# Seven half-size products in place of eight in the first feed-forward matmul of a transformer block

## The chip, the cores and the metric

The kernel runs on one core of a Trainium2 chip. Its time is the device time of one execution in microseconds (us). Five engines of the core work side by side, each with an instruction queue of its own: TensorE (PE: matrix products; PEld: the loads of its stationary operand), VectorE (DVE), ScalarE (ACT), GpSimd (POOL), and SyncE (SP), which here issues the transfers between DRAM and the on-chip memory SBUF. Products are summed in PSUM, eight banks of 128 partitions by 512 numbers of four bytes.

## The reference, cut to what matters

The program is two transformer blocks on 512 tokens of width 1024. The part that changes is at the end of the second block:

```python
D_MODEL = 1024; SEQ = 512; D_FF = 4 * D_MODEL

def second_block(x, c, ..., w1, w2, w_ada, b_ada):
    ...
    x = x + gt1 * (mixed @ w_o[l])
    h = rmsnorm_2(x, g_norm2[l]) * (1.0 + sc2) + sh2
    x = x + gt2 * (jnp.square(jax.nn.relu(h @ w1[l])) @ w2[l])
    return x
```

So `h` is 512 x 1024, `w1` is 1024 x 4096 and `w2` is 4096 x 1024. The product `h @ w1` is the first feed-forward product.

## The kernel before, in words

All dense products are made to float32 accuracy from operands split in two: `split` (L130) copies a raw tile into a type with fewer bits (`act.copy`, ScalarE, L131), the high part, and subtracts it from the raw one (L128), the low part; the subtraction is on GpSimd by default, or on VectorE. `mm3` (L149) then issues three matmuls per 128 rows of the contraction: high by high, high by low, low by high (L150 to L152).

The second block keeps the tokens in columns: the normed input `h` lies as `hh`/`hl`, eight slices of 128 channels by 512 tokens, in tiles of the tags `QK` (high) and `PT` (low). The stage around the change runs so:

- `rows_second` (L694) ends the attention's output product for the second half of the tokens. Its last weight tiles use the buffers `wh`/`wl`, of which there are three each; raw weights land in `wr`, four buffers. In its middle, `col_norm` (L657) transposes the normed first half of the tokens on TensorE (L664), scales and shifts it (L668 on ScalarE, L670 on VectorE), and splits it (L672, L673).
- `norm2` (L1095) adds the residual to the second half (L1104, L1105), sums squares (L1106), forms the root (L157 to L161) and scales the rows (L1110) into four tiles of the tag `T`, which has five buffers.
- Meanwhile TensorE multiplies the first half of the tokens, 256 columns, with four of the first `EARLY` = 5 weight tiles (`first_half`). A weight tile is 1024 rows by 128 columns of `w1`: 8 x 3 = 24 matmuls. Then it transposes the second half, multiplies the fifth tile with the first half, and all five with the second half.
- The other 27 weight tiles are run whole, 512 columns, by `mtile` (L389); after each, `hid_out` (L1132) applies Relu and Square on ScalarE and writes the result to `hid`, 32 slices of 128 by 512, which are kept for the second product. Every second tile, `ada_step` (L257) does one step of the modulation vector on VectorE (L217, two operations on 512 KB of `w_ada`).

```python
    def hid_out(ft, srcs):
        t1 = tmp([128, 512])
        n = 512 // len(srcs)
        for i, ps in enumerate(srcs):
            s = slice(n * i, n * i + n)
            act.activation(t1[:, s], ps[:, :n], AF.Relu)
        act.activation(hid[ft], t1, AF.Square)
```

The order on TensorE is that of the program's text. The other engines' queues are ordered by a planner when the program is built: it takes the operation that is ready first by its own costs, and among ready ones the one that stands first in the text. All queues are worked off in order. Tiles of one tag share that tag's buffers; a tile waits until an earlier one's last reader is done. A bank of PSUM (`bank()`, eight) is treated as one thing: a write waits for reads of the same bank that stand before it.

Of the kernel before, what the change touches and what calls it, by code (L numbers as in the profile page):

```python
# [16 lines left out]
D = 1024  # L17
# [34 lines left out]
def hybrid_then_adaln_block(ctx, tc, a, out, tap=None):  # L52
# [1038 lines left out]
    h3h = [wt([128, 4, 512], "QK", F32R) for _ in range(2)]  # L1091
    h3l = [wt([128, 4, 512], "PT", F32R) for _ in range(2)]
# [22 lines left out]
    for t in range(4):  # L1115
        x = resid.tile([128, D], F32, name="xr", tag="xr", bufs=4)
        sp.dma_start(x, y1_d[128 * t:128 * t + 128, :])
        xr.append(x)
    us = norm2(hts[0], pss_o)
    pss = rows_second(hts[1], a["w_o_2"], x_of, kept2,  # L1120
                      lambda: col_norm(hts[0], us, h3h, h3l, scl[:, 2, :], mod[:, 24:32]))
    us = norm2(hts[1], pss)
    if tap: tap("x2", xr[2]); tap("h3", f(h3h[1][:, 1, :]))
    hh, hl = h3h, h3l

    hid = []
    for tag, n in [("PT", 1), ("V", 1), ("Y", 4), ("h", 2)]:
        for _ in range(n):
            t = wt([128, 4, 512], tag) if tag != "h" else hpool.tile([128, 4, 512], F32, name="hid", tag="h", bufs=4)
            hid += [t[:, q, :] for q in range(4)]  # L1130

    def hid_out(ft, srcs):  # L1132
        t1 = tmp([128, 512])
        n = 512 // len(srcs)
        for i, ps in enumerate(srcs):
            s = slice(n * i, n * i + n)
            act.activation(t1[:, s], ps[:, :n], AF.Relu)
        act.activation(hid[ft], t1, AF.Square)
# [3 lines left out]
    EARLY = 5  # L1142
    w1y = [wt([128, 2, KT, 128], "Y", F32R) for _ in range(2)]
    first = [weights([wcols(w1x, FF, 128 * ft, 128)], [KT, 128],
                     *((w1y[0][:, ft], w1y[1][:, ft]) if ft < 2 else (None, None))) for ft in range(EARLY)]
    halves = [bank() for _ in range(EARLY)]

    def first_half(ft, q):
        for k in range(KT):
            h, l = h_of(k, 256 * q, 256)  # L1150
            mm3(halves[ft][:, 256 * q:256 * q + 256], first[ft][0][:, k, :], first[ft][1][:, k, :], h, l, k == 0, k == KT - 1)
# [79 lines left out]
```

## Time and profile before

| | |
|---|---|
| three runs | 1066.61, 1068.08, 1071.96 us; median 1068.08 us |
| the profiled execution | 1064.9 us |
| its span, from the first to the last instruction | 1063.1 us |
| TensorE, its weight loads | busy 1027.0 us (97%), 845.1 us (79%) |
| VectorE, ScalarE, GpSimd | busy 527.6, 527.2, 309.2 us |
| mean granted clock of TensorE | 0.997 |

"Busy" is the time in which an engine has an instruction under way. Matmuls overlap: a row of 256 columns lasts 0.28 us, but the next one starts earlier, so the cost of one is read from the starts. Times within the trace count from the start of the span. "Granted clock" is the share of TensorE's full clock, 2.4 GHz, that it was given: 1.00 or 0.50.

### The profile page before, as it was taken

Reading aid. Unit: us, or ns where it says so; the run is one execution under the profiler, and the core shown is the slowest. Engines: PE = TensorE matmul, PEld = TensorE weight load, DVE = VectorE, ACT = ScalarE, POOL = GpSimd, SP = SyncE. Lnnn points to the kernel's source line nnn. Section 1 sums busy time; section 2 is a strip of 40 time slices with the busy share of each in tenths; the row PEclk is TensorE's granted clock in tenths of the full one; section 3 lists DMA queues with packets and bytes.
Section 4 is the critical chain, followed back from the end, with each engine's and each line's share of the span. In section 5 each row is a group of like instructions: output and inputs, shape, how many; then the busy total and the mean of one; then the engine's idle time right before and its main releaser. Section 6 shows DMA issues by size and latency. Waiting matters only on the chain.

```text
span 1063.1 us, 14244 instructions
## 1 busy us (share of the span) xinstructions
PE 1027.0 (97%) x5431; PEld 845.1 (79%) x5431; DVE 527.6 (50%) x1017; ACT 527.2 (50%) x990; POOL 309.2 (29%) x163
## 2 busy tenths in 40 slices
PE   7999999999999998999899988999999999999998
PEld 6987987778888887987678766798888888888886
DVE  5375866873534478368777587471131003121115
ACT  6365654554544554566687686354433433222221
POOL 4221123423332552112212115113322333323330
PEclk9999999999999999999999999999999999999999
DMA  8342532454633656236412235434445233233312
GB/s 239 84 119 64 151 114 80 139 141 121 175 98 95 237 160 210 71 99 165 134 50 61 70 107 151 156 100 119 119 122 153 82 100 113 87 99 97 100 60 80
DMA packets 133976, 125.48 MB, mean 118 GB/s; under 512 B 6054, under 2 KB 110338, under 8 KB 133907
## 3 DMA queue, kind: packets, MB, share of 16 engines
q1 hardware_dynamic: 133906, 124.56, 39.8%
q8 instruction: 43, 0.70, 0.3%
q14 instruction: 27, 0.21, 0.1%
HBM read 119.82 MB, written 4.73 MB: 117 GB/s over the span
## 4 chain that ended last, share of the span: by engine, by line
PE 79%; DVE 10%; issue 3%; ACT 3%; DMA 3%; POOL 1%; SPq 0%; DVEq 0%; POOLq 0%; ACTq 0%
PE ps L150 24%; PE ps L152 23%; PE ps L151 23%; PE ps L963 2%; DMA wr<-in_w_in_dram 2%; DVE ada L217 1%; PE ps L519 1%; PE ps L438 1%; PE ps L916 1%; PE ps L439 1%; PE ps L234 1%; DVE QK L427 1%; DMA wr<-in_w_ada_dram 1%; ACT wh L131 1%; PE ps L664 1%
## 5 line engine op out<-in xcount | busy, mean ns | idle before, releaser
L128 POOL TENSOR_TENSOR wl<-wr,wh 128x1024 fp32r<-128x1024 f32 x105 | 255.6, 2436 | 625.2 <-ACT wh L131 618.9
L131 ACT CAST wh<-wr 128x1024 fp32r<-128x1024 f32 x142 | 148.8, 1048 | 292.2 <-PE ps L151 140.6
L150 PE MATMUL ps<-hh,wh 128*128 128x512 f32 (+1 forms) x352 | 129.4, 368 | 0.3 <-DVE nmx L483 0.3
L151 PE MATMUL ps<-hl,wh 128*128 128x512 f32 (+1 forms) x352 | 124.9, 355 | 0.0
L152 PE MATMUL ps<-hh,wl 128*128 128x512 f32 (+1 forms) x352 | 124.6, 354 | 0.0
L217 DVE SCALAR_TENSOR_TENSOR ada<-wr,vc,ada 128x512 f32<-128x512 f32 x84 | 83.6, 995 | 39.4 <-DMA wr<-in_w_ada_dram 38.2
L152 PE MATMUL ps<-wh,T 128*128 128x512 f32 x256 | 100.9, 394 | 0.0
L150 PE MATMUL ps<-wh,T 128*128 128x512 f32 x256 | 100.8, 394 | 0.0
L151 PE MATMUL ps<-wl,T 128*128 128x512 f32 x256 | 100.5, 392 | 0.0
L150 PE MATMUL ps<-QK,wh 128*128 128x512 f32 (+1 forms) x264 | 99.3, 376 | 0.0
L151 PE MATMUL ps<-PT,wh 128*128 128x512 f32 (+1 forms) x264 | 98.6, 373 | 0.0
L152 PE MATMUL ps<-QK,wl 128*128 128x512 f32 (+1 forms) x264 | 98.4, 373 | 0.0
L128 DVE TENSOR_TENSOR wl<-wr,wh 128x1024 fp32r<-128x1024 f32 x37 | 45.2, 1222 | 89.9 <-ACT wh L131 89.9
L150 PEld LDWEIGHTS ps<-hh,wh 128*128 128x128 f32 x352 | 66.2, 188 | 20.0 <-issue 10.8
L152 PEld LDWEIGHTS ps<-hh,wl 128*128 128x128 f32 x352 | 66.2, 188 | 9.6
L151 PEld LDWEIGHTS ps<-hl,wh 128*128 128x128 f32 x352 | 66.3, 188 | 7.7
L152 PEld LDWEIGHTS ps<-QK,wl 128*128 128x128 f32 x264 | 49.6, 188 | 9.8
L150 PEld LDWEIGHTS ps<-QK,wh 128*128 128x128 f32 x264 | 49.6, 188 | 9.7 <-ACT T L668 0.2
L151 PEld LDWEIGHTS ps<-wl,T 128*128 128x128 f32 x256 | 48.1, 188 | 11.3
L152 PEld LDWEIGHTS ps<-wh,T 128*128 128x128 f32 x256 | 48.1, 188 | 11.3
L151 PEld LDWEIGHTS ps<-PT,wh 128*128 128x128 f32 x264 | 49.7, 188 | 9.1
L150 PEld LDWEIGHTS ps<-wh,T 128*128 128x128 f32 x256 | 48.1, 188 | 10.9
(332 smaller groups left out, 2215.2 us busy)
## 6 DMA issues: line engine op xcount, KB each, us to landing
wr<-in_w_in_dram SPq DMA_DIRECT2D x64, 512.0 KB, 5.0
wr<-in_w_dram SPq DMA_DIRECT2D x64, 512.0 KB, 4.0
wr<-in_w_ada_dram SPq DMA_DIRECT2D x48, 512.0 KB, 3.8
wr<-in_w_out_dram SPq DMA_DIRECT2D x12, 512.0 KB
wr<-in_w_o_dram SPq DMA_DIRECT2D x12, 512.0 KB, 3.6
xr<-in_x_dram SPq DMA_DIRECT2D x8, 512.0 KB, 3.8
wr<-in_w_up_pool_dram SPq DMA_DIRECT2D x8, 256.0 KB, 3.0
wr<-in_w_up_attn_dram SPq DMA_DIRECT2D x8, 256.0 KB
```

Source lines behind the costliest of these rows:

```text
L128: (eng or pool).tensor_tensor(dst, raw, f(hi), op=OP.subtract)
L131: act.copy(dst_hi, raw)
L150: pe.matmul(ps, lh, rh, start=start, stop=False)
L151: pe.matmul(ps, lh, rl, start=False, stop=False)
L152: pe.matmul(ps, ll, rh, start=False, stop=stop)
L217: dve.scalar_tensor_tensor(acc, raw[:, q, :], cs, acc, op0=OP.mult, op1=OP.add)
L234: pe.matmul(ps[:, j:j + 1], acc[:, 128 * j:128 * j + 128], ones_f[:, :1], start=True, stop=True)
L427: dve.scalar_tensor_tensor(A[e][other], src[own], scale, f(A[e][own]), op0=OP.mult, op1=OP.subtract)
L438: pe.matmul(ps, A[e][:, sa], B[e][:, sb], start=True, stop=False)
L439: pe.matmul(ps, A[e][:, sa], L[e][:, sb], start=False, stop=stop)
L519: pe.matmul(po[64 * e:64 * e + 64, c0:], lhs, rhs, start=j < 0, stop=j == 3)
L963: pe.matmul(ps[:, d0:], ntri if j2 == j else nones, part[:, SOFF[j2]:SOFF[j2] + 512 - d0], start=False, stop=part is sl and j2 == j, skip_ ...
```

## The change

The product of two neighbouring weight tiles with `h` becomes a 2 by 2 block product. The blocks of the weights are the two halves of the contraction (512 rows each, `H0` and `H1` of a raw tile) for two tiles `ra` and `rb`; the blocks of `h` are the two halves of its channels by the two halves of its tokens (`b11`, `b12`, `b21`, `b22`, each 512 channels by 256 tokens). Winograd's form of Strassen's scheme needs seven block products in place of eight. For that, sums of blocks are formed: s1 to s4 of the weights, per pair (`sums`), and t1 to t4 of `h`, once (`wino_right`). Each sum is split into high and low part as the operands were before.

One block product is `prod`: four slices of the contraction, three matmuls each, 256 columns. Per pair there are `firsts` (the two products of the unchanged tile `ra` with b11 and b21, in the two halves of one bank), `middles` (s2 by t2 and s3 by t3 onto the first half of that bank, `x`; s1 by t1 into another bank, `y`) and `lasts` (a22 by t4 onto x, s4 by b22 onto y), which is issued one pair later. Between them partial sums are copied to `hid` by ScalarE and added there by VectorE. Relu and Square follow in `lasts`. `firsts` of pairs 0 to 3 take the place of the first halves, then `wino_right` follows, then `firsts` of pairs 4 and 5. The raw tiles `ra` of pairs 0 to 5 are fetched a second time for `sums`. `first_row` makes its low parts on GpSimd, `sums` and `wino_right` on VectorE. `ada_step` is called once per pair.

```diff
-    h3h = [wt([128, 4, 512], "QK", F32R) for _ in range(2)]
-    h3l = [wt([128, 4, 512], "PT", F32R) for _ in range(2)]
...
+    b32 = wt([128, KT, 256], "V")
+    left = [wt([128, KT, 256], tag, F32R) for tag in ("QK", "PT")]
...
+    def col_quads(tts, t):
+        for b in (0, 2, 1, 3):
+            ps = bank().rearrange("p (k n) -> p k n", k=2)
+            for q in range(2):
+                k = 2 * b + q
+                for i, tt in enumerate(tts):
+                    pe.transpose(ps[:, q, 128 * i:128 * i + 128], t[i][k // 4][:, 128 * (k % 4):128 * (k % 4) + 128], ident)
+            yield b, ps
+
+    def scaled(dst, ps, b):
+        for q in range(2):
+            k = 2 * b + q
+            g, c = scl[:, 2, k:k + 1], mod[:, 24 + k:25 + k]
+            if q:
+                act.activation(dst[:, q, :], ps[:, q, :], AF.Identity, scale=g, bias=c)
+            else:
+                dve.tensor_scalar(dst[:, q, :], ps[:, q, :], g, c, op0=OP.mult, op1=OP.add)
+
+    def wino_left(t):
+        for b, ps in col_quads(hts[0], t):
+            o = (slice(None), slice(2 * b, 2 * b + 2))
+            scaled(b32[o], ps, b)
+            act.copy(left[0][o], b32[o])
+            dve.tensor_tensor(left[1][o], b32[o], f(left[0][o]), op=OP.subtract)
...
+    def wino_right(t):
...
+        def cut(name, g, src, eng=None):
+            hi, lo = right[name][0][g], right[name][1][g]
+            act.copy(hi, src)
+            (eng or dve).tensor_tensor(lo, src, f(hi), op=OP.subtract)
+
+        for b, ps in col_quads(hts[1], t):
+            x = got[b] = tmp([128, 2, 256])
+            scaled(x, ps, b)
+            if b < 2:
+                continue
+            g = b - 2
+            b12, b22 = got[g], x
+            b11, b21 = b32[:, 2 * g:2 * g + 2, :], b32[:, 4 + 2 * g:6 + 2 * g, :]
+            t1, t2 = (wt([128, 2, 256], "Z") for _ in range(2))
+            t3, t4 = (wt([128, 2, 256], "PTm") for _ in range(2))
+            dve.tensor_tensor(t1, b12, b11, op=OP.subtract)
+            dve.tensor_tensor(t2, b22, t1, op=OP.subtract)
+            cut("t2", g, t2)
+            cut("t1", g, t1)
+            dve.tensor_tensor(t3, b22, b12, op=OP.subtract)
+            cut("t3", g, t3)
+            dve.tensor_tensor(t4, b21, t2, op=OP.subtract)
+            cut("t4", g, t4)
+            cut("b22", g, b22)
...
+    def prod(ps, w, name, first):
+        for k in range(4):
+            wh, wl = (x[:, 128 * k:128 * k + 128] for x in w)
+            bh, bl = b_of(name, k)
+            go = dict(skip_group_check=True)
+            pe.matmul(ps, wh, bh, start=first and k == 0, stop=False, **go)
+            pe.matmul(ps, wh, bl, start=False, stop=False, **go)
+            pe.matmul(ps, wl, bh, start=False, stop=k == 3, **go)
+        clk[0] += 1420
...
-    for ft in range(EARLY - 1):
-        first_half(ft, 0)
-    col_norm(hts[1], us, h3h, h3l, scl[:, 2, :], mod[:, 24:32])
-    first_half(EARLY - 1, 0)
-    for ft in range(EARLY):
-        first_half(ft, 1)
-        hid_out(ft, [halves[ft]])
+    EARLY = 6
+
+    def w1_raw(ft):
+        raw = wts.tile([128, D], F32, name="wr", tag="wr", bufs=4)
+        sp.dma_start(raw.rearrange("p (k n) -> p k n", k=KT), wcols(w1x, FF, 128 * ft, 128))
+        return raw
+
+    def w_pair(n, tag_hi="wh", tag_lo="wl"):
+        if n == 1024:
+            return wts.tile([128, n], F32R, name="wh", tag="wh", bufs=3), wts.tile([128, n], F32R, name="wl", tag="wl", bufs=3)
+        return wt([128, n], "Z", F32R), wt([128, n], "PTm", F32R)
...
+    def first_row(ra):
+        w = w_pair(1024)
+        split(*w, ra, pool)
+        return [[x[:, s] for x in w] for s in (H0, H1)]
+
+    def sums(ra, rb):
+        u, v, w = w_pair(1024), w_pair(1024), w_pair(512)
+        s1, s2, s3, s4 = (tmp([128, 512]) for _ in range(4))
+        dve.tensor_tensor(s1, rb[:, H0], rb[:, H1], op=OP.add)
+        dve.tensor_tensor(s2, s1, ra[:, H0], op=OP.subtract)
+        dve.tensor_tensor(s3, ra[:, H0], rb[:, H0], op=OP.subtract)
+        dve.tensor_tensor(s4, ra[:, H1], s2, op=OP.subtract)
+        cuts = [[x[:, h] for x in y] for y in (u, v) for h in (H0, H1)]
+        for c, x in zip(cuts, (s2, s1, s3, s4)):
+            split(*c, x, dve)
+        split(*w, rb[:, H1], dve)
+        return [w] + cuts
+
+    def plus(dst, kept, other):
+        act.copy(dst, kept)
+        dve.tensor_tensor(dst, other, dst, op=OP.add)
...
+    def firsts(i, row):
+        X[i] = bank()
+        prod(X[i][:, :256], row[0], "b11", True)
+        prod(X[i][:, 256:], row[1], "b21", False)
+        plus(hid[2 * i][:, :256], X[i][:, :256], X[i][:, 256:])
+
+    def middles(i, ws):
+        a22, s2, s1, s3, s4 = ws
+        x = X[i][:, :256]
+        prod(x, s2, "t2", False)
+        act.copy(hid[2 * i][:, 256:], x)
+        y = bank()[:, :256]
+        prod(y, s1, "t1", True)
+        prod(x, s3, "t3", False)
+        plus(hid[2 * i + 1][:, 256:], x, y)
+        tails.append((i, x, y, a22, s4))
+
+    def lasts():
+        if not tails:
+            return
+        i, x, y, a22, s4 = tails.pop()
+        prod(x, a22, "t4", False)
+        prod(y, s4, "b22", False)
+        act.activation(hid[2 * i + 1][:, :256], x, AF.Relu)
+        dve.tensor_tensor(hid[2 * i][:, 256:], y, hid[2 * i][:, 256:], op=OP.add)
+        two = both(i)
+        act.activation(two[:, :512], two[:, :512], AF.Relu)
+        act.activation(two[:, 768:], two[:, 768:], AF.Relu)
+        act.activation(two, two, AF.Square)
...
+    for i in range(EARLY - 2):
+        firsts(i, first_row(w1_raw(2 * i)))
+    wino_right(us)
+    for i in range(EARLY - 2, EARLY):
+        firsts(i, first_row(w1_raw(2 * i)))
...
-    for ft in range(EARLY, 32):
-        if ft == 31:
+    for i in range(16):
+        ra, rb = w1_raw(2 * i), w1_raw(2 * i + 1)
+        if i >= EARLY:
+            firsts(i, first_row(ra))
+        ws = sums(ra, rb)
+        lasts()
+        middles(i, ws)
+        ada_step()
+        if i == 15:
             w2_operands()
-        run(mtile(128 * ft, [(0, 512)], w1x, FF, lambda _, ps: hid_out(ft, [ps])))
-        if ft % 2 == 0:
-            ada_step()
+    lasts()
```

## Rows read from the trace of the kernel before

**Rows 1.** The page, section 1: engine, busy us, share of the span, instructions.
```profile
PE 1027.0 (97%) x5431; PEld 845.1 (79%) x5431; DVE 527.6 (50%) x1017; ACT 527.2 (50%) x990; POOL 309.2 (29%) x163
```
**Rows 2.** Busy time by stretch: start:end, length, each engine's busy us (instructions), clock, DMA.
```profile
697.97:709.37 11.40, 11.40 (x98) 11.39 (x97) 9.84 (x22) 4.68 (x13) 2.41 (x1) 1.00 0.35 98
709.37:711.20 1.83, 1.83 (x18) 1.67 (x16) 1.19 (x3) 0.61 (x2) 0.00 (x0) 1.00 0.87 231
711.20:728.20 17.00, 17.00 (x144) 17.00 (x144) 3.29 (x6) 10.20 (x17) 3.82 (x2) 1.00 0.06 9
728.20:880.75 152.55, 152.55 (x669) 123.83 (x668) 25.71 (x25) 59.19 (x82) 49.23 (x21) 1.00 0.42 122
```
**Rows 3.** The chain of waits from 690 to 740 us, shares by line.
```profile
by line: PE ps L151 31.4%; PE ps L150 31.4%; PE ps L152 31.0%; PE ps L664 7.0%
```
**Rows 4.** Timeline of TensorE (256 columns) and of ScalarE's weight copies: start, us, what.
```profile
711.43 0.29 PE L151 MATMUL ps<-PT,wh 128*128 128x256 f32 x1
...
728.20 0.28 PE L151 MATMUL ps<-PT,wh 128*128 128x256 f32 x1
...
869.62 1.05 ACT L131 CAST wh<-wr 128x1024 fp32r<-128x1024 f32 x1 [3.37 <-PE ps L151]
...
875.19 1.05 ACT L131 CAST wh<-wr 128x1024 fp32r<-128x1024 f32 x1 [3.36 <-PE ps L151]
```
**Rows 5.** Groups by line, 698 to 880.7 us, last row from 1050: busy us, mean ns.
```profile
L128 POOL TENSOR_TENSOR wl<-wr,wh 128x1024 fp32r<-128x1024 f32 x23 | 55.5, 2411 | 128.7 <-ACT wh L131 128.7
L151 PEld LDWEIGHTS ps<-PT,wh 128*128 128x128 f32 x264 | 49.7, 188 | 9.1
L131 ACT CAST wh<-wr 128x1024 fp32r<-128x1024 f32 x30 | 31.5, 1049 | 93.3 <-PE ps L151 92.0 <-PE ps L152 1.2
L1137 ACT ACTIVATE T<-ps 128x512 f32<-128x512 f32 x31 | 18.3, 592 | 4.2 <-PE ps L152 4.2
L673 DVE TENSOR_TENSOR PT<-T,QK 128x512 fp32r<-128x512 f32 x4 | 2.6, 688 | 0.9 <-ACT QK L672 0.9
...
L1205 DVE TENSOR_TENSOR ot<-ps,PTm 128x256 f32<-128x256 f32 x2 | 0.8, 419 | 0.0
```
**Rows 6.** Timeline of VectorE and GpSimd in the norm and at the stage's end.
```profile
698.01 1.28 DVE L1105 TENSOR_TENSOR xr<-T,xr 128x512 f32<-128x512 f32 x2
700.50 1.23 DVE L1107 TENSOR_TENSOR jn<-jn,jn 128x1 f32<-128x1 f32 x1
702.32 0.67 DVE L1105 TENSOR_TENSOR xr<-T,xr 128x512 f32<-128x512 f32 x1
705.98 0.88 DVE L1110 TENSOR_SCALAR T<-xr,jr 128x512 f32<-128x512 f32 x2
710.01 1.90 DVE L670 TENSOR_SCALAR T<-ps,scl,mod 128x256 f32<-128x256 f32 x4 [1.97 <-PE ps L664]
712.15 1.29 DVE L673 TENSOR_TENSOR PT<-T,QK 128x512 fp32r<-128x512 f32 x2 [0.24 <-ACT QK L672]
877.28 1.99 DVE L128 TENSOR_TENSOR T<-PT,T 128x512 fp32r<-128x512 f32 x1 [10.93 <-ACT T L131]
...
699.31 2.41 POOL L128 TENSOR_TENSOR wl<-wr,wh 128x1024 fp32r<-128x1024 f32 x1 [4.78 <-ACT wh L131]
876.32 2.40 POOL L128 TENSOR_TENSOR wl<-wr,wh 128x1024 fp32r<-128x1024 f32 x1 [3.18 <-ACT wh L131]
```
**Rows 7.** TensorE after a wait in an earlier stage: timeline, and busy time by stretch.
```profile
422.71 0.44 PE L664 MATMUL ps<-ident,PTm 128*128 128x128 f32 x1 [2.87 <-DVE PTm L733]
...
422.80:426.20 3.40, 3.40 (x17) 3.40 (x18) 2.63 (x6) 1.72 (x4) 0.00 (x0) 0.50 0.70 274
```
**Rows 8.** Timeline of VectorE: one modulation step.
```profile
737.41 1.54 DVE L217 SCALAR_TENSOR_TENSOR ada<-wr,vc,ada 128x512 f32<-128x512 f32 x2 [4.64 <-DMA wr<-in_w_ada_dram]
```

More of the change, by code (lines that the diff above doesn't have):

```diff
@@ new lines, in pieces @@
+    def pieces(name, hi, lo):
+        right[name] = (hi, lo)
+    def wino_right(t):
+        for names, tags in ((("b22", "t1"), ("QK", "PT")), (("t2", "t3"), ("h", "h"))):
+            hl_ = [wt([128, 8, 256], tag, F32R) if tag != "h" else hpool.tile([128, 8, 256], F32R, name="tsum", tag="h", bufs=4)
+                   for tag in tags]
+            for i, name in enumerate(names):
+                pieces(name, *([x[:, 4 * i + 2 * g:4 * i + 2 * g + 2, :] for g in range(2)] for x in hl_))
+        pieces("t4", *([LZ[i][g][:, :512].rearrange("p (k n) -> p k n", k=2) for g in range(2)] for i in range(2)))
+        got = {}
+        def cut(name, g, src, eng=None):
[21 more added lines that the diff above has]
+            cut("b22", g, b22)
@@ new lines, in b_of @@
+    def b_of(name, k):
+        if name in ("b11", "b21"):
+            return tuple(x[:, k + (4 if name == "b21" else 0), :] for x in left)
+        return tuple(x[k // 2][:, k % 2, :] for x in right[name])
+    def prod(ps, w, name, first):
[7 more added lines that the diff above has]
+        clk[0] += 1420
@@ L1119, in hybrid_then_adaln_block @@
     us = norm2(hts[0], pss_o)
     pss = rows_second(hts[1], a["w_o_2"], x_of, kept2,
-                      lambda: col_norm(hts[0], us, h3h, h3l, scl[:, 2, :], mod[:, 24:32]))
+                      lambda: wino_left(us))
     us = norm2(hts[1], pss)
[L1123 to L1127, printed above, removed]
+    if tap: tap("x2", xr[2])
+    hid, hid_t = [], []
+    for tag, n in [("PT", 1), ("Y", 2), ("V", 1), ("Y", 2), ("h", 2)]:
@@ L1128, in hybrid_then_adaln_block @@
         for _ in range(n):
             t = wt([128, 4, 512], tag) if tag != "h" else hpool.tile([128, 4, 512], F32, name="hid", tag="h", bufs=4)
+            hid_t.append(t)
             hid += [t[:, q, :] for q in range(4)]
[L1132 to L1138, printed above, removed]
@@ L1140, in hybrid_then_adaln_block @@
     dve_turn[0] = TURN2
     w1x = a["w1_2"]
[L1142 to L1151, printed above, removed]
@@ new lines, in hybrid_then_adaln_block @@
+    H0, H1 = slice(0, 512), slice(512, 1024)
+    def first_row(ra):
[14 more added lines that the diff above has]
+        return [w] + cuts
@@ new lines, in plus @@
+    def plus(dst, kept, other):
+        act.copy(dst, kept)
+        dve.tensor_tensor(dst, other, dst, op=OP.add)
+    X, tails = {}, []
+    def firsts(i, row):
[13 more added lines that the diff above has]
+        tails.append((i, x, y, a22, s4))
@@ L1160, in hybrid_then_adaln_block, with both @@
+    def both(i):
+        return hid_t[i // 2].rearrange("p q n -> p (q n)")[:, 1024 * (i % 2):1024 * (i % 2) + 1024]
+    for i in range(EARLY - 2):
[3 more added lines that the diff above has]
+        firsts(i, first_row(w1_raw(2 * i)))
     todo += [(5, k) for k in range(8)]
```

1 line of the change is left out of this document (added).

## The prediction

> **What bounds the kernel now.** I read the page first: TensorE is busy 97% of the span, VectorE 50% [rows 1]. That is a mean over stages, so I then cut the span around the first feed-forward product. It fills the stretch from 697.97 us to 880.75 us, 182.8 us, and in its four pieces TensorE is busy for every microsecond while VectorE has slack: 9.84 of 11.40 us in the first piece, but only 25.71 of 152.55 us in the last [rows 2]. The chain of waits around the start of this stage consists of the matmul lines and the transposes alone [rows 3]. So here time is the number of matmuls times their step. What the reader is to see for the change: whatever it takes off TensorE counts in full, but only as long as VectorE, which today does nearly nothing in the long piece, can feed it.
>
> **The change, part by part.** Durations are from the one profiled execution: 1064.9 us, of which 1063.1 us are the span. The median of the three runs shown is 1068.1 us, 3.2 us (0.3%) above it. I make the sum on the execution and put the difference onto the median.
>
> *The matmuls.* A matmul of 256 columns follows the one before by 0.119 us: from 711.43 to 728.20 us there are 141 steps, 16.77 us [rows 4]. At 512 columns, one weight tile of 24 matmuls takes 875.19 - 869.62 = 5.57 us, 0.232 us each [rows 4]. Before, the stage has 5 tiles in halves (240 x 0.119 = 28.6 us) and 27 whole ones (27 x 5.57 = 150.4 us), together 179.0 us; the other 3.8 us are transposes and the small products of the modulation, which stay. After, each of 16 pairs has 7 products of 4 x 3 = 12 matmuls at 256 columns: 16 x 84 x 0.119 = 159.9 us. TensorE gains **19.1 us**. This is the whole gain of the change; all else takes from it.
>
> *The norm ahead of the transposes.* Before, only one of the weight tiles' low parts was made on GpSimd while VectorE did `norm2` of the second half (at 699.31 us). Now `first_row` sends every one to GpSimd. A buffer `wh`/`wl` comes free when the third-last product ends, at about 695.2, 698.0, 700.8, 703.7 and 706.5 us, so five of them, 2.41 us each [rows 5], stand nearly end to end from 697.0 to about 711 us. An add on VectorE with both inputs in SBUF waits while GpSimd runs one: L1107, 0.14 us of work, took 1.23 us, until GpSimd was through at 701.72 us; L128 on 512 columns took 1.99 us in place of 0.69, until GpSimd was through at 878.72 us [rows 6]. `norm2` has a dozen such operations. If each turn of VectorE is followed by one of GpSimd, the last residual add comes at about 711.5 us in place of 702.99; 3.9 us lie between that and the end of L1110 today (706.86 [rows 6]), less what the other row tile already did, 0.8: 714.6 us. TensorE reaches the transposes at 709.37 us, so it waits 5.2 us; earlier in the kernel a wait of 2.87 us was followed by 3.40 us at a granted clock of 0.50 [rows 7], and at half clock sixteen transposes, 1.83 us now [rows 2], take some 1.5 us more. The lower end is 0, if VectorE gets several operations in at each turn, as the two L1105 at 698.01 us did [rows 6]; the upper 6.7. I take 4, because L1107 shows the full wait.
>
> *The operand sums `wino_right`.* This is the largest new cost. Before, the second half of the rows needed four operations L670 and four L673 on VectorE, and matmuls covered them. Now, per half of the contraction (two halves): 2 scalings at 0.45 us, 4 sums and 5 low parts at 0.60 us. The steps are those between two operations of one row: two L673 take 1.29 us, one 0.69, so one step is 0.60; four L670 take 1.90, so some 0.45 [rows 5, 6]. That is 6.3 us a half and 12.6 us in all, from 0.6 us after the transposes begin (X): X + 13.2, and about 0.6 us more for waits on ScalarE's copies. Then come the adds of `firsts` 4 and 5 (2 x 0.33) and, for the first product of `middles(0)`, s1 to s4 and the low part of s2 (5 x 0.60): X + 17.5. The sums can't be made much earlier, since T has five buffers, four of which hold the normed rows until the transposes and then the four scaled blocks. TensorE has 1.83 us of transposes and 48 matmuls (5.7 us) as cover: X + 7.5. It waits **10 us**. Below: if the order of VectorE were ideal, it still has 18.0 us to do (12.6 + 9 x 0.60) before `lasts(0)`, for which TensorE has 11.8 us of cover: 6.2. Above: a GpSimd operation that falls into it (2.4) and half clock for 3.40 us (1.7) make 14. I take 10.
>
> *Six pairs without their own first products.* For pairs 0 to 5 `firsts` is done, so TensorE has 60 x 0.119 = 7.1 us a pair. VectorE has 9 x 0.60, two adds out of PSUM (256 columns take 0.42 us, 0.33 as a step [rows 5]) and one modulation step (1.54 us for two L217 [rows 8]): 7.6 us. It lags 0.5 us a pair, 2.5 us over five; the wait before gives it a small lead: 0 to 4 us, I take 2. Transfers carry it: 3 x 0.52 MB in 7.1 us are 220 GB/s, while 274 GB/s were moved in one stretch [rows 7]. The six first tiles that are fetched twice (3 MB on SP's queue) lie in idle time of that queue.
>
> *Ten full pairs.* TensorE has 10.0 us. VectorE: 9 x 0.60 + 3 x 0.33 = 6.4 us, plus up to 2.4 us behind GpSimd's one low part, 8.8. ScalarE: a copy of 1024 (0.95 as a step), five of 512 (0.52), three of 256 (0.31), then Relu 256, 512, 256 and Square 1024: 6.6 us, from L131 and L1137 [rows 5], with 256 columns taken as 0.37 to 0.40 us by the slope between 512 and 1024. Neither is full, so what counts is order. The tightest place: x is copied out between the s2 and the s3 product into the same bank, and the s1 product, 1.43 us, goes to another bank meanwhile. In ScalarE's queue that copy stands behind what `lasts` of the pair before still has to do, Relu 512 and Square, which end some 2.2 to 2.6 us after `middles` begins; the s3 product is due at 2.85 and the copy takes 0.4. So 0 to 0.3 us a pair are lost. No row shows such a copy; its bounds are nothing and, were it done after the s1 product in each pair, 1 us. I take 0.2 x 10 = 2 us (0 to 10).
>
> Sum: -19.1 + 4 + 10 + 2 + 2 = -1.1 us, 1063.8 us on the execution and **1067 us** on the median. With all lower ends it is -12.9 us (1055), with all upper ones +15.6 us (1084).
>
> **The rivals.** *The stalls are half of that (faster).* Every term has its lower end in a row or in a bound: VectorE gets its operations in between GpSimd's (0), `wino_right` costs 6 to 8, the pairs 0 to 2. For it: the two L1105 that were not held, and that a planner, not the text, orders the queues of VectorE and ScalarE. Against it: 18.0 us of VectorE work against 11.8 us of cover can't be reordered away. Time: -19.1 + 8 to 10, so 1057 to 1059 us.
>
> *The copy out of x's bank paces every pair (slower).* Place: between the s2 and s3 products. If ScalarE's queue has the copies of s3, s4 and a22 (3 x 0.52) and the second Relu (0.31) there too, the order of the text, Square ends 3.45 us after `middles` began, the copy at 3.85, and TensorE waits 1.0 us. Price: 16 x 1.0 us in place of my 4 for the pairs: +11 us, 1079 us. It decides from the point where the copy begins more than 2.45 us after `middles`. For it: pairs 0 to 5 leave VectorE no slack, and the add before the Relu comes late then. Against it: s3's buffer may come free before `lasts`, and the copies be done by then. The Trainium skill (PSUM — Partial Sum Buffer, Summary: rules for kernel authors) tells authors to read PSUM from another bank than the one a matmul writes. By it alone each of the 32 reads, x's and that of `firsts`, would stop the products for its 0.37 us, an estimate of 12 us; no row here shows two products of one bank with a read between them.
>
> *The change does not do what it says:* a matmul of 256 columns on the new operands takes longer than 0.119 us. From 11.14 / 84 = 0.133 us on nothing is left. Against it: 0.119 us is shown for 0.188 us weight loads that lie beside the matmuls [rows 5], and the new ones have the same shape. Its time, with my stalls, is 1086 us.
>
> **How the numbers follow.** A measurement here tells about 0.5% (5.3 us) from no change, so same is 1062.8 to 1073.4 us. My forecast has 0.42, and its own range is 1061 to 1074. The faster rival has 0.31. The slower one has 0.25 and the last 0.02: 0.27 for slower. The range that is to hold 8 in 10 must reach into both: 1055, all lower ends, to 1080, the pacing copy.
>
> **What would show it.** Right: matmuls of 256 columns, 1344 of them between the norm and the second product, 0.119 us apart; a gap of TensorE ahead of the transposes behind L1105, L1110 and GpSimd's L128; the longest gap, near 10 us, at the first product of `middles(0)`, released by VectorE; then a stage that is nearly closed, with VectorE over 90% busy in pairs 0 to 5 and near 70% after. The stage should last about 182 us. Wrong: no gap at the transposes (the lock costs nothing); gaps at each s3 product with ScalarE as the releaser (the second rival); or TensorE closed from `middles(0)` on and a stage near 170 us (the first).

## The result, and the profile after

The changed kernel takes 1083.4 us (median of 4 runs, 1083.07 to 1085.27) against 1068.2 us (4 runs), a ratio of 1.0141 with a 95% interval of 1.0112 to 1.0170: 15 us slower. The forecast was 1067 us, the range 1055 to 1080, so the prediction was wrong.

The profiled execution took 1085.27 us with a span of 1083.6 us. The page, section 1, answers to [rows 1]:

```profile
PE 1018.5 (94%) x5887; PEld 861.9 (80%) x5887; DVE 637.3 (59%) x1215; ACT 573.0 (53%) x1108; POOL 296.1 (27%) x155
```

TensorE has less to do than before, 1018.5 us in place of 1027.0, and is idle more. The busy time by stretch (the columns of [rows 2]; the stage now lasts from 701.51 to 901.70 us) shows where:

```profile
701.51:714.11 12.60, 11.76 (x97) 11.54 (x96) 12.21 (x20) 6.84 (x17) 6.67 (x3) 1.00 0.40 111
714.11:723.05 8.94, 1.92 (x19) 1.68 (x17) 3.75 (x9) 2.41 (x7) 4.67 (x2) 0.85 0.52 145
723.05:739.18 16.13, 7.78 (x48) 7.58 (x49) 14.91 (x27) 9.63 (x20) 0.00 (x0) 0.71 0.11 31
739.18:787.90 48.72, 44.79 (x344) 43.27 (x345) 43.69 (x73) 31.67 (x61) 2.40 (x1) 0.95 0.59 173
787.90:901.70 113.80, 106.34 (x875) 105.27 (x874) 76.41 (x128) 72.60 (x135) 31.15 (x11) 0.99 0.39 112
901.70:1083.60 181.90, 177.68 (x770) 144.21 (x768) 42.08 (x59) 48.15 (x61) 52.88 (x22) 1.00 0.30 93
```

The stage takes 200.2 us in place of 182.8. What follows it is unchanged: 181.9 us, and 1063.1 - 880.75 = 182.35 before. In the second row TensorE does its sixteen transposes (1.9 us of 8.94) and stands. VectorE is idle there as well, busy 3.75 us, so it is not short of time but stopped. In the third and fourth it is full: 14.91 of 16.13, 43.69 of 48.72 us.

The waits of TensorE in the stage (engine, tile and line that waited, releaser: us in total, times, longest):

```profile
PE ps L1197 <- ACT wh L131: 8.4, 1, 8.4
PE ps L1197 <- ACT T L1138: 7.0, 1, 7.0
PE ps L1197 <- DVE V L1253: 3.9, 1, 3.9
PE ps L1199 <- POOL wl L128: 3.5, 2, 2.6
PE ps L1197 <- ACT Y L1252: 1.5, 2, 1.1
```

The first is the wait ahead of `middles(0)`, which I had expected. The second, behind the transposes, I had not. The timeline of VectorE (start, us, what, [idle before <- releaser]) shows what it hangs on; `firsts(4)` waits for a PSUM bank that the scalings L1138 and L1140 have to read first:

```profile
713.44 0.88 DVE L1108 TENSOR_SCALAR T<-xr,jr 128x512 f32<-128x512 f32 x2
...
715.65 0.42 DVE L1253 TENSOR_TENSOR Y<-ps,Y 128x256 f32<-128x256 f32 x1 [0.79 <-ACT Y L1252]
720.33 0.49 DVE L215 TENSOR_SCALAR ada<-wr,vc 128x512 f32<-128x512 f32 x1 [4.25 <-DMA wr<-in_w_ada_dram]
720.86 0.75 DVE L217 SCALAR_TENSOR_TENSOR ada<-wr,vc,ada 128x512 f32<-128x512 f32 x1
...
721.86 1.44 DVE L1140 TENSOR_SCALAR T<-ps,scl,mod 128x256 f32<-128x256 f32 x3
```

The norm ends at 714.3 us, in time. But ahead of the scalings VectorE's queue holds a modulation step, L215, whose transfer is not there: 4.25 us idle, and the scalings come at 721.86. In the program's text this step is called behind `middles(0)`; the planner had put it ahead of the scalings. SyncE's timeline shows the transfer issued only at 716.61 us, behind five weight loads for which the four `wr` buffers had to come free:

```profile
694.16 17.57 SPq L1221 DMA_DIRECT2D wr<-in_w_dram  x5
716.61 0.37 SPq L207 DMA_DIRECT2D wr<-in_w_ada_dram  x1
```

I cut the stage into blocks: 24 matmuls of `firsts` or `lasts` last 2.86 us, 36 of `middles` 4.28, and what a block takes longer, or lies between two, is lost. 200.2 us are 159.9 of products, 1.9 of transposes and 38.4 lost. My sum held 19.9: 18 of stalls and 1.9 of small modulation products.

| place | forecast | lost |
|---|---|---|
| norm, up to the transposes: a wait of `firsts(3)` for GpSimd's low part | 4 | 1.1 |
| behind the transposes: wait 7.0, then half clock in `firsts(4)` 1.9 | 0 | 8.9 |
| ahead of `middles(0)`: wait 8.5, then half clock and a wait of 0.4 in it 2.75 | 10 | 11.3 |
| rest of pairs 0 to 5, 0.9 of it foreseen small products | 2 + 0.9 | 6.0 |
| full pairs, 1.0 of it foreseen small products | 2 + 1.0 | 11.0 |

The 11.0 us are not spread out: 6.4 lie at pair 6 and 2.9 at pair 11. Pairs 12 to 14 last 9.97 us each with TensorE busy throughout, the 84 steps of 0.119 and nothing else:

```profile
853.95:863.92 9.97, 9.97 (x86) 9.97 (x85) 6.85 (x13) 7.04 (x13) 2.71 (x1) 1.00 0.37 107
```

### The profile page after: what moved, and what is told of

Same layout as the page of the kernel before. It is cut to its first block, busy times and chain, and to the rows that moved or that the text cites. A ratio compares the mean times of both kernels' runs of the same rounds, so it can differ in the third digit from the quotient of the medians.

```text
span 1083.6 us, 15531 instructions
## 1 busy us (share of the span) xinstructions
PE 1018.5 (94%) x5887; PEld 861.9 (80%) x5887; DVE 637.3 (59%) x1215; ACT 573.0 (53%) x1108; POOL 296.1 (27%) x155
## 5 line engine op out<-in xcount | busy, mean ns | idle before, releaser
L128 POOL TENSOR_TENSOR wl<-wr,wh 128x1024 fp32r<-128x1024 f32 x99 | 248.1, 2508 | 678.3 <-ACT wh L131 584.6
L131 ACT CAST wh<-wr 128x1024 fp32r<-128x1024 f32 x128 | 134.1, 1048 | 204.8 <-issue 90.0
L217 DVE SCALAR_TENSOR_TENSOR ada<-wr,vc,ada 128x512 f32<-128x512 f32 x84 | 78.6, 936 | 4.9 <-DMA wr<-in_w_ada_dram 3.9
L1197 PE MATMUL ps<-QK,wh 128*128 128x256 f32 x256 | 74.1, 289 | 7.0 <-ACT T L1138 7.0
L1199 PE MATMUL ps<-QK,wl 128*128 128x256 f32 x256 | 73.8, 288 | 3.5 <-POOL wl L128 3.5
L1198 PE MATMUL ps<-PT,wh 128*128 128x256 f32 x256 | 73.8, 288 | 0.0
L128 DVE TENSOR_TENSOR wl<-T,wh 128x512 fp32r<-128x512 f32 x64 | 44.7, 728 | 23.0 <-ACT wh L131 23.0
L152 PEld LDWEIGHTS ps<-wh,T 128*128 128x128 f32 x256 | 48.1, 188 | 11.3
L150 PE MATMUL ps<-h2h,wh 128*128 128x512 f32 (+1 forms) x144 | 54.4, 378 | 0.0
L128 DVE TENSOR_TENSOR wl<-wr,wh 128x1024 fp32r<-128x1024 f32 x29 | 35.4, 1222 | 30.2 <-ACT wh L131 30.2
```

The source lines that it names most:

```text
L128: (eng or pool).tensor_tensor(dst, raw, f(hi), op=OP.subtract)
L131: act.copy(dst_hi, raw)
L150: pe.matmul(ps, lh, rh, start=start, stop=False)
L152: pe.matmul(ps, ll, rh, start=False, stop=stop)
L217: dve.scalar_tensor_tensor(acc, raw[:, q, :], cs, acc, op0=OP.mult, op1=OP.add)
L1197: pe.matmul(ps, wh, bh, start=first and k == 0, stop=False, **go)
```

## Experiments

The stage is compared in the profiled executions from the first product to the first one of the second feed-forward product. It is that of one execution, the time is a median, and the executions of a kernel differ by some us (e2: 1080.9 to 1088.5 us), so stage and time do not differ by the same amount. The trace of e1 is from the longest of its five executions (1081.2 us), that of e2 from the shortest of four, that of e14 from the longest of twelve. The one kernel with two traces, e18 and e20, gave stages of 177.7 and 177.6 us. Each ratio is to runs of the kernel before on the same chip, whose medians lay between 1067.7 and 1068.2 us.

| kernel | median us | ratio to before (95%) | stage us |
|---|---|---|---|
| before | 1068.2 | | 182.8 |
| changed | 1083.4 | 1.0141 (1.0112 to 1.0170) | 200.2 |
| e1 steps from pair 6 | 1074.4 | 1.0070 (1.0050 to 1.0091) | 192.4 |
| e2 order of lasts | 1085.7 | 1.0166 (1.0134 to 1.0198) | 198.4 |
| e3 no low parts | 1084.9 | 1.0152 (1.0119 to 1.0186) | 198.0 |
| e5 no sums | 1073.7 | 1.0067 (1.0043 to 1.0091) | 187.9 |
| e4b fillers | 1086.9 | 1.0171 (1.0141 to 1.0202) | 202.6 |
| e6 = e1 + e2 | 1079.2 | 1.0091 (1.0062 to 1.0120) | 195.3 |
| e8 = e1 + e3 | 1070.3 | 1.0022 (0.9994 to 1.0050) | 182.8 |
| e10 = e6, gate copy later | 1078.2 | 1.0087 (1.0056 to 1.0118) | 193.6 |
| e11 steps in second attention | 1074.6 | 1.0054 (1.0033 to 1.0074) | 182.5 |
| e12 = e11 + e2 | 1067.6 | 1.0005 (0.9986 to 1.0023) | 177.5 |
| e13 = e12, 60 fillers | 1069.4 | 1.0011 (0.9995 to 1.0028) | 180.2 |
| e16 = e12, 84 fillers | 1068.7 | 1.0009 (0.9991 to 1.0027) | 177.8 |
| e15 = e12, sums by need | 1068.6 | 1.0012 (0.9994 to 1.0030) | 178.7 |
| e14 before, steps in attention | 1072.3 | 1.0037 (1.0019 to 1.0054) | 180.9 |
| e18 = e12, steps in first half | 1064.8 | 0.9975 (0.9959 to 0.9992) | 177.7 |
| e17 = e18 + e15 | 1066.0 | 0.9980 (0.9966 to 0.9995) | 178.4 |
| e19 before, steps in first half | 1068.3 | 1.0011 (0.9995 to 1.0027) | 180.9 |
| e20 = e18 again | 1064.6 | 0.9977 (0.9962 to 0.9992) | 177.6 |

**e1: the modulation steps from pair 6 on.**

```diff
         middles(i, ws)
-        ada_step()
+        if i >= EARLY:
+            ada_step()
```

> One edit: the modulation steps begin with pair 6 in place of pair 0. Theory: in the changed kernel the first of them stands ahead of the scalings of the transposed rows in VectorE's queue and waits for a transfer that got its buffer late, so that TensorE waits 7.0 us after the transposes and then loses 1.9 us at half clock; without it that gap is below 1.5 us, and the full pairs, which lost 4.0 and 2.3 us around pair 6, lose no more than that. Time 1083.4 - 9 to 13, about 1072 us. Rival: the wait after the transposes is one for the norm and for PSUM banks, and the modulation step only stood in it: the gap stays over 5 us and the time over 1080 us.

9.0 us less than the changed kernel: the low end of the theory. The wait behind the transposes falls from 7.0 to 1.5 us, the half clock in `firsts(4)` is gone, and from pair 1 to pair 9 TensorE stops for little more than the hand-over of x's bank. But the profiled execution loses 10.1 us in pairs 10 to 12; the steps now lie in pairs 6 to 13:

```profile
PE ps L1197 <- ACT wh L131: 9.9, 1, 9.9
PE ps L1197 <- DVE hid L1253: 5.0, 1, 5.0
```

The wait of 5.0 us is that of `middles(12)`. VectorE's timeline ahead of it, with GpSimd's row: a weight tile that comes late, then a modulation step and a low part that lasts as long as one of GpSimd's, in front of the add that `middles(12)` needs:

```profile
850.55 0.69 DVE L1241 TENSOR_TENSOR T<-wr 128x512 f32<-128x512 f32 x1 [2.71 <-DMA wr<-in_w_dram]
...
852.49 0.75 DVE L217 SCALAR_TENSOR_TENSOR ada<-wr,vc,ada 128x512 f32<-128x512 f32 x1
853.15 2.83 DVE L128 TENSOR_TENSOR wl<-T,wh 128x512 fp32r<-128x512 f32 x1
855.91 0.41 DVE L1253 TENSOR_TENSOR hid<-ps,hid 128x256 f32<-128x256 f32 x1
...
852.58 2.86 POOL L128 TENSOR_TENSOR wl<-wr,wh 128x1024 fp32r<-128x1024 f32 x1 [10.41 <-DVE T L1243]
```

**e2: lasts behind the middles of the next pair.** After `middles` come the `lasts` of the same pair in x's bank, and in pairs 0 to 5 no product lies between: x has to be copied out first, 0.62 us a pair. The edit puts the next `middles` between.

```diff
-        lasts()
-        middles(i, ws)
+        if 0 < i < EARLY - 1:
+            middles(i, ws)
+            lasts()
+        else:
+            lasts()
+            middles(i, ws)
```

(`lasts` then takes the oldest entry of `tails`.)

> One edit: in pairs 1 to 4 the last two products of the pair before come after middles in place of ahead of it, so that the copy of x out of its bank has other products beside it. Theory: the five gaps of 0.62 to 1.24 us between middles and lasts (3.3 us in all) are the wait for that copy, and go: 1080 us. Rival: VectorE paces pairs 0 to 5 (7.6 us of work against 7.1), and the gaps only move to the start of middles: 1083 us.

The rival. The hand-overs are gone, but the stage is only 1.8 us shorter and the time is not: the same waits stand at other places, now for VectorE and for ScalarE's copies.

**e3: without ten low parts in `wino_right`.** The operands t1 to t4 and b22 use their high part twice.

```diff
             act.copy(hi, src)
-            (eng or dve).tensor_tensor(lo, src, f(hi), op=OP.subtract)
+            right[name][1][g] = hi
```

> Left out: the ten low parts of t1 to t4 and b22 (the products read the high part in their place). VectorE has 10 x 0.60 = 6.0 us less between the transposes and the first s2 product. Theory: the 8.5 us gap there is VectorE's work, and shrinks to about 3 us, with 1 to 2 us less at half clock behind it: 1083.4 - 6 to 8, about 1076 us. Rival: the gap is set by the weight sums of pair 0, which wait for their raw tiles or buffers: it stays over 7 us, time over 1081 us.

The time is the rival's, but its reason is not: the wait ahead of `middles(0)` shrinks from 8.4 to 1.5 us, as the theory had it, so VectorE's work does set it. What it gives is paid again in pairs 2, 4, 7 and 11. In pair 2 the copy of x (L1269) is late because ScalarE, too, stands at a weight tile whose transfer is not there.

```profile
PE ps L1199 <- ACT T L1138: 7.0, 1, 7.0
PE ps L1201 <- POOL wl L128: 3.4, 2, 2.6
PE ps L1199 <- ACT Y L1269: 3.4, 2, 2.4
PE ps L1199 <- DVE V L1255: 2.4, 1, 2.4
PE ps L1199 <- ACT V L1269: 1.9, 1, 1.9
PE ps L1199 <- ACT wh L131: 1.5, 1, 1.5
```

ScalarE's timeline in pair 2:

```profile
755.30 0.62 ACT L131 CAST Z<-wr 128x512 fp32r<-128x512 f32 x1 [3.78 <-DMA wr<-in_w_dram]
...
757.45 0.35 ACT L1269 COPY Y<-ps 128x256 f32<-128x256 f32 x1
```

**e5: without any sum.** The t operands are blocks of rows split as they are, and the weights are split whole on GpSimd; products and bank traffic stay.

```diff
         for b, ps in col_quads(hts[1], t):
             x = tmp([128, 2, 256])
             scaled(x, ps, b)
+            cut("t1" if b < 2 else "b22", b % 2, x)
...
+        split(*u, ra, pool)
+        split(*v, rb, pool)
```

> Left out: all sums, of the weights (the two raw tiles of a pair are split whole, low parts on GpSimd) and of the rows (t1 to t4 are replaced by split blocks of the rows); the 84 products a pair, the partial sums out of PSUM and the modulation steps stay. Theory: TensorE's gain of 19 us is real, and the sums cost the 8.5 us gap, most of the 2.75 us behind it and some 5 us in the pairs; the 9 us at the transposes and 3 us of hand-offs stay: 1083.4 - 16, about 1067 us. Rival: products of half size bring no gain even when fed: 1078 us or more.

Between the two. VectorE's busy time in the stage falls from 151 to 59 us, and the stage still loses 26 us, 9.1 of them behind the transposes, where the changed kernel lost 8.9. VectorE stands in the modulation steps, whose transfers come late without any sums in the way:

```profile
DVE ada L217 <- DMA wr<-in_w_ada_dram: 13.7, 5, 4.3
```

So the steps cost by the wait for their transfers even where VectorE has time for their arithmetic.

**e6, e8, e10: what is left when the steps are late.** e6 and e8 put e1 together with e2 and with e3. e10 is e6 with the gate row's copy and write a pair later (in `ada_end`, a third stage for the gate of the last modulation).

> The changed kernel with the modulation steps from pair 6 on, and in pairs 1 to 4 the lasts of the pair before behind the middles. Each alone: 1074.4 (steps late) and 1085.7 (order). Theory (the hand-over of x's bank costs TensorE 0.62 us a pair, and the order alone gained nothing because VectorE, with the modulation steps, had no time left): with the steps gone VectorE has slack, and the five hand-overs of pairs 0 to 4 go: 5 x 0.62 = 3.1 us less than 1074.4, about 1071. Rival (VectorE paces these pairs with or without the steps): within 1 us of 1074.4, the same waits under other names.

> The changed kernel with the modulation steps from pair 6 on and the ten low parts of t1 to t4 and b22 left out (the low operand is the high one again), which is part of the computation. Left out in the changed kernel, the low parts gained nothing in time, though the wait ahead of the first middles fell from 8.5 to 1.7 us. Theory (the 6.9 us were given back because VectorE had the modulation steps ahead of it in pairs 0 to 6): here they stay, and the time is 5 to 8 us under 1074.4, about 1068. Rival (the sums of the pairs are what paces VectorE; any start of the middles that is earlier is waited for later): within 2 us of 1074.4.

> The kernel with late modulation steps and the changed order, and the gate row's copy out of PSUM, with its write to DRAM, issued a pair later than its transpose. In the trace with late steps VectorE waited 4.0 us for that transpose, SyncE had no weight load under way meanwhile, and the middles of pair 12 then waited 5.1 us. Theory (that write stands ahead of the weight loads on SyncE's queue and makes them late): 3 to 6 us less than the same kernel without this edit, about 1067. Rival (a slip of the modulation steps' own loads, which the edit does not touch): within 1 us of it.

e8 is nearer to its theory's 5 to 8 us than to the rival's 2: the same low parts that gained nothing before now gain 4.1 us in the medians (the two intervals just meet, at 1.0050), and the wait ahead of `middles(0)` is 2.7 us in place of 9.9. So the theory of VectorE's work in `wino_right` was right; the modulation steps had covered it. e6 missed: the five hand-overs are gone, but 5.1 us are lost at pair 7, and the 5.0 us at pair 12 remain; its interval overlaps e1's, so that it is slower is not shown. e10 missed too: the wait at pair 12 is still 4.9 us, so the gate's write is not its cause.

**e11, e12, e14: the steps out of the stage.** They are issued behind those of the second attention, in e14 in the kernel before.

```diff
-    todo += [(v, k) for v in (4, 2) for k in range(8)]
+    todo += [(v, k) for v in (4, 2, 5) for k in range(8)]
...
-    todo += [(5, k) for k in range(8)]
```

> The changed kernel with the eight modulation steps of the last gate taken out of the stage: they are issued behind the sixteen steps of the second attention, ahead of the stage. Theory (the steps cost the stage twice: in pairs 0 to 5 by VectorE's queue, 9.0 us, and, moved to pairs 6 to 13, by the weight buffers, where the trace with late steps lost 10.1 us in pairs 10 to 13): 6 to 9 us less than the 1074.4 of the late steps, about 1067; their 12 us of VectorE work lie in the attention, where VectorE was busy 65 to 77% of the time. Rival (the attention cannot hide them, since VectorE's softmax steps pace it): as much is paid there as is saved, 1074 to 1080.

> The kernel with the modulation steps ahead of the stage, and in pairs 1 to 4 the lasts of the pair before behind the middles. Theory (the order's 3.1 us were lost again in pair 7 of the kernel with late steps, because loads of the steps and of the weights share four buffers): with no step in the stage they stay, 3 us less than the kernel without the order, about 1064. Rival (the pairs are paced by VectorE or by the weight loads at any order): within 1 us of it.

> The kernel before with the same move of the eight modulation steps into the second attention. It tells what the move is worth without the change. Theory (in the kernel before, TensorE's 512-column products set the pace of the stage and VectorE has time left for the steps): within 2 us of 1067.7. Rival (the steps cost that stage too): 4 to 8 us less, about 1062.

The whole stage of the changed kernel, of e11, of e12 and, with the move, of the kernel before:

```profile
701.51:901.70 200.19, 172.59 (x1378) 169.34 (x1377) 150.96 (x253) 123.16 (x235) 44.89 (x17) 0.95 0.43 122
```
```profile
708.06:890.57 182.51, 167.05 (x1361) 164.69 (x1360) 135.10 (x234) 124.18 (x235) 42.67 (x17) 0.96 0.40 111
```
```profile
702.87:880.32 177.45, 164.46 (x1362) 163.15 (x1360) 136.12 (x234) 123.86 (x235) 42.72 (x17) 0.97 0.40 114
```
```profile
710.33:891.24 180.91, 180.91 (x906) 152.11 (x904) 23.76 (x36) 74.67 (x113) 55.16 (x23) 1.00 0.32 89
```

In e11 the stage is 17.7 us shorter, though VectorE does only 16 us less and had 49 us to spare. In the kernel before the same removal shortens it by 1.9 us (182.8 to 180.9), which is what the steps' small products take of TensorE. These are VectorE's waits for transfers in the changed kernel, up to 800 us:

```profile
DVE T L1241 <- DMA wr<-in_w_dram: 6.1, 5, 2.5
DVE ada L215 <- DMA wr<-in_w_ada_dram: 4.3, 1, 4.3
```

In e11 it no longer waits for a transfer at all, and TensorE's waits of the stage are down to the one ahead of `middles(0)`, a rest behind the transposes, the hand-overs and two of 0.8 and 0.4 us for low parts:

```profile
PE ps L1197 <- ACT wh L131: 9.8, 1, 9.8
PE ps L1197 <- ACT T L1138: 1.5, 1, 1.5
PE ps L1197 <- ACT Y L1252: 1.4, 3, 0.5
```

e12 takes the five hand-overs as well, 3.1 us by their waits; its stage is 5.0 us shorter than e11's, 1.4 of it a shorter stretch at half clock in `middles(0)`, and its median 7.0 us, more than the theory's 3. So e2's theory holds where VectorE is not stopped. The time of e11 does not follow its stage: 1074.6 us, the e1 figure, so the theory of that run failed and its rival holds: the attention pays. e14 shows the same in the kernel before, 4.1 us more (1.0037), where I had expected none. An estimate of the price, the median less the stage: 885.4 us lie outside the stage before, 891.4 in e14, 892.1 in e11, so some 6 us in both.

**e4b, e13, e16: the half clock.** Products of 256 columns that feed nothing fill TensorE's wait ahead of `middles(0)` (e4b also behind the transposes).

```diff
+        if i == 0:
+            for q in range(60):
+                pe.matmul(y, left[0][:, 0, :128], left[0][:, 0, :], start=q == 0, stop=q == 59)
         prod(x, s2, "t2", False)
```

> The changed kernel with two times 60 extra products of 256 columns that feed nothing: one lot on TensorE's queue behind the transposes of wino_right, one ahead of the first middles. At 0.119 us each they take 7.1 us, a little less than the two waits of 8.9 and 8.5 us in which they stand. Theory (the half clock that follows a wait is a price of its own): TensorE is no longer idle, the clock stays at 1.00 through firsts 4 and middles 0, and the 1.91 and 2.75 us that these lose go; the 1.91 comes back as a longer wait ahead of middles 0, so some 3 to 5 us less than the changed kernel's 1083.4, about 1079.5. Rival (VectorE sets the pace of pairs 0 to 5, whatever TensorE's clock): the wait moves into the pairs behind, and the time stays within 1.5 us of 1083.4.

> The same with 60 products of 256 columns that feed nothing ahead of the first middles, 7.1 us in a wait of about 10. Theory (the half clock behind that wait is a price of its own): middles 0 lose nothing in place of 2.4 us, and the time is 2 to 3 us less than the same kernel without them, about 1062. Rival (what follows waits for VectorE anyway): within 1 us of it.

> The kernel with the modulation steps ahead of the stage and the changed order, and 84 products of 256 columns that feed nothing ahead of the first middles: 10.0 us at 0.119, all of the wait, where 60 left 2.9 us idle and the clock fell all the same. Theory (the half clock behind the wait is a price of its own): the clock stays at 1.00, middles 0 lose nothing in place of 2.1 us, and the time is about 2 us under 1067.6, 1065.5. Rival (VectorE's data would not have been there sooner): the 2.1 us come back as waits inside pairs 0 to 2, and the time is within 1 us of 1067.6.

e4b missed both forecasts. Its first lot needs nothing but old operands and the bank of `firsts(4)`, and it waited the same 7.0 us and then ran on top of it; so it is the bank for which `firsts(4)` waits (L1261 is the filler):

```profile
PE ps L1261 <- ACT T L1138: 7.0, 1, 7.0
```

Ahead of `middles(0)` its clock stayed at 1.00, but these began late. The 60 of e13 left 2.9 us of the wait open; the clock fell behind that, the third row has a mean of 0.57. The stage is 2.7 us longer than e12's; the time is 1.8 us above e12's, which the intervals do not tell from none:

```profile
726.06:733.20 7.14, 7.14 (x62) 7.14 (x60) 7.14 (x14) 5.19 (x10) 0.00 (x0) 1.00 0.00 0
733.20:736.07 2.87, 0.21 (x2) 0.01 (x1) 2.87 (x7) 1.24 (x3) 0.00 (x0) 0.97 0.00 0
736.07:743.82 7.75, 7.39 (x36) 7.09 (x37) 5.92 (x10) 2.67 (x5) 0.00 (x0) 0.57 0.61 159
```

The 84 of e16 fill it, and the clock stays at 1.00 in the wait and in `middles(0)`:

```profile
729.85:739.91 10.06, 10.06 (x86) 10.06 (x85) 10.06 (x19) 6.48 (x13) 0.00 (x0) 1.00 0.00 0
739.91:745.15 5.24, 4.59 (x38) 4.34 (x36) 5.24 (x10) 2.64 (x5) 0.00 (x0) 1.00 0.77 203
```

Yet pairs 0 and 1 lose 0.95 + 0.12 + 1.43 = 2.5 us in waits for low parts on VectorE, where e12 lost 2.1 in `middles(0)`, nearly all of it to the clock. The rival, by the time and by the stage (177.8 against 177.5 us): with VectorE busy all of the wait and all of `middles(0)`, the half clock there costs nothing of its own.

**e15: pair 0's sums in the order of need.** Each sum is split as soon as it is made; the last t4 and b22 come behind the sums of the `middles`.

```diff
+        if early:
+            split(*cuts[0], s2, dve)
+            split(*cuts[1], s1, dve)
         dve.tensor_tensor(s3, ra[:, H0], rb[:, H0], op=OP.subtract)
+        if early:
+            split(*cuts[2], s3, dve)
         dve.tensor_tensor(s4, ra[:, H1], s2, op=OP.subtract)
+        if early:
+            rest0.pop()()
```

> The kernel with the modulation steps ahead of the stage and the changed order, and for pair 0 alone VectorE's work in the order in which the middles need it: each sum is split as soon as it is made, the last t4 and b22 (five VectorE operations of about 0.6 us) come behind the three sums of the middles. Theory (VectorE's queue sets the 10.0 us ahead of the first middles): four or five operations of 0.6 us stand less ahead of them, so that they start 2 to 3 us earlier; with pair 1's middles between, the last t4 and b22 are in time, and the time is 2 to 3 us under 1067.6, about 1065. Rival (VectorE's sum of work in pairs 0 and 1 is what counts, in any order): the wait moves to the products behind, and the time is within 1 us of 1067.6.

The rival again: `middles(0)` start 1.35 us earlier, and 1.14 us ahead of `middles(1)` and 1.0 inside them come back. So VectorE's sum of work counts, as the rival had it, and not this order.

**e18, e17, e19, e20: a cheap place for the steps.** e18 is e12 with the eight steps behind those of the first half (`(0, 1, 3, 5)` in the first list, `(4, 2)` in the second), where the up projections run.

> The kernel with the changed order, and the eight modulation steps issued not in the second attention but behind those of the first half, where the first half's up projections run and VectorE is busy 18 to 33 us of 50. In the kernel before, the move into the second attention cost 4.1 us. Theory (that price is the attention's, where VectorE works on the softmax that TensorE waits for): among the up projections the steps cost 0 to 1 us, and the time is 3 to 4 us under 1067.6, about 1064. Rival (the steps cost the same wherever they share the four weight buffers): within 1 us of 1067.6.

> The changed order, the modulation steps among the up projections of the first half, and pair 0's sums in the order of need. If the theories of both parts hold, their gains of 2.5 and 3.5 us add: about 1062, faster than the kernel before (1068.2) by 0.5% or a little more. If VectorE's work counts in any order, or the steps cost as much in either place, about 1064 to 1068.

> The kernel before, with its eight modulation steps issued among the up projections of the first half, as in the fastest version of the changed kernel (1064.8). Theory (TensorE's products set the pace of the old stage, which hides the steps): within 2 us of 1068.1, so that what is left of the gain, 2 to 4 us, is the change's own with its two repairs. Rival (the move alone is worth the 3 us): about 1065, and the change then brings nothing.

> The changed kernel with the changed order and the modulation steps among the up projections of the first half once more, beside the kernel before with the same move: 1064.8 again, 2 to 4 us under that, if the gain is the change's; the same time as that, if it is the move's.

As the theory had it, but for e17, where only the move's gain shows. Two sets of runs of e18 give 0.9975 (0.9959 to 0.9992) and 0.9977 (0.9962 to 0.9992): faster than the kernel before by 0.2%. The move alone, in the kernel before, brings nothing (1.0011, 0.9995 to 1.0027). So the 3.7 us between 1068.3 and 1064.6 are the change's own once its two repairs are in; the stages differ by 3.2 to 3.3 us. Of the 15.9 us that e18's stage still loses, 12.5 lie ahead of and in `middles(0)`.

## Why the prediction was wrong, point by point

**The gain on TensorE was right.** 19.1 us were forecast; the steps are 0.119 us on all new operands and a full pair lasts 9.97 us. That a matmul takes longer is refuted.

**The step that failed** is "Six pairs without their own first products", with its sentence "Transfers carry it". I priced a modulation step at its 1.54 us of VectorE [rows 8], took 2 us for these pairs, and had no term for a step ahead of them; 8.9 us were lost behind the transposes at the first one, which the sum put at nothing. The step is also an entry in an in-order queue that waits for a transfer, and a third customer of the four `wr` buffers. The row I read had 4.64 us of idle time in front of L217 for that very transfer; before, nothing waited behind it. In the changed kernel the transposes' scalings, the sums and the adds do. The eight steps cost its stage 17.7 us (e11) and that of the kernel before 1.9. Of the 17.7, 1.9 are their small products on TensorE. That a kernel without them takes 182.5 us, where my sum said 181.7, is in part luck: by the places of the table e11 loses 1.1, 1.6, 13.6, 3.9 and 0.5 us, so `wino_right` and the hand-overs cost more than I had, and the norm and the full pairs less.

**The first term** (norm behind GpSimd, 4) was too high. VectorE's adds do stand while GpSimd works, two L1103 took 4.79 us beside two low parts where two L1105 had taken 1.28 [rows 6]. But three low parts fell into the stretch and not five, and the norm was in time; the 1.1 us are `firsts(3)` at its own low part. What came late was the step behind the norm.

```profile
700.56 5.23 POOL L128 TENSOR_TENSOR wl<-wr,wh 128x1024 fp32r<-128x1024 f32 x2 [2.48 <-ACT wh L131]
701.55 4.79 DVE L1103 TENSOR_TENSOR xr<-T,xr 128x512 f32<-128x512 f32 x2
```

**`wino_right`, 10,** was right in its wait: 8.5 us in the changed kernel, 10.0 with the steps away, set by VectorE's work (the releaser in the trace is ScalarE's copy L131 of a sum that VectorE makes): fewer operations shorten it (e3, e8); another order shortens it by 1.35 us, which come back behind it (e15). The half clock and short wait behind it, 2.75 and 3.6 us, come on top. Its cover was not as I had counted it, since `firsts(4)` waits for a bank that the scalings free.

**The hand-over of x's bank** to `lasts`, 0.62 us in pairs 0 to 5, I had overlooked; I had looked at the copy ahead of the s3 product. With the steps out, that copy stopped TensorE once, for 0.14 us (e11), so the rival of the pacing copy falls. The Trainium skill (PSUM — Partial Sum Buffer, Summary: rules for kernel authors) tells authors to read PSUM from another bank than the one a matmul writes. The 12 us that I had estimated from it are not seen: a full pair of 9.97 us, 84 steps of 0.119, has no room for a stop at each read, and the measurement decides. Where the next product does go to the bank that is read, it costs the 0.62 us.

**The rival of half the stalls** falls as well: in the changed kernel no term but the norm's came out below my value.

**The ten full pairs** lost 11.0 us, 2 + 1.0 of it foreseen. 2.9 us at pair 11 are a wait for GpSimd's low part; at pair 6 it is VectorE behind a weight tile that came 2.5 us late. Both are gone in e11. That the steps' loads alone make the tiles late, rather than their order among the loads, was not separated.

One thing stays open: why e6, with fewer stops in its first pairs, was no faster than e1 (its trace shows 5.1 us at pair 7, not the reason why it is that pair).

## What to carry to other kernels

A small operation in an engine's queue holds up all that is queued behind it for as long as it waits for its data; when a change fills that engine, look first for idle time with a DMA as the releaser in its old timeline, and move such operations to a stretch where the engine has slack (here that, with the changed order of `lasts`, turned 1.4% slower into 0.2% faster). A repair that gains nothing alone may be hidden behind another wait: e2 and e3 showed their gain only once the steps were late or gone. When the work of one product is spread over three engines, sum each engine's work between two fixed points, then count everything that shares its buffers.

## What the runs showed of the hardware

In e13 TensorE stood for most of 2.9 us behind 7.1 us of filling products, and over the next 7.75 us its clock was granted at a mean of 0.57, that is mostly at 1.2 GHz. In e16, with products in all of that wait, it stayed at 1.00 over the next 5.24 us. The times, 1069.4 and 1068.7 us beside e12's 1067.6, do not differ by more than their intervals: VectorE was busy in all of e16's two stretches, 10.06 and 5.24 us, and it set the pace. So before a stretch at half clock is counted as a loss, the row of the same stretch should be read for an engine that would have been late anyway.
